# Sparse attention projections in 256, 456 and 512 columns, with merged head operations, in a two-layer hybrid trunk

## The chip, the cores and the metric

The kernel runs on one core of one Trainium2 chip. The metric is the device time in microseconds of one execution. In the profile TensorE is PE (its weight loads are PEld), VectorE is DVE, ScalarE is ACT, GpSimd is POOL and SyncE is SP. DRAM is reached by DMA queues that SP and POOL feed.

## What is computed

Two layers over 512 tokens of width 1024 in float32. In each layer one projection of the normalised input, `h @ w_in`, feeds a gated convolution, a sparse attention, a gated recurrence and a cross attention into 256 memory tokens; their outputs are lifted to width 1024, gated, added and projected, and a feed-forward block follows. The change touches the sparse attention (8 heads of 64, one key and value head, an indexer of 8 heads of 64 that picks 128 keys for each token):

```python
topk = min(TOPK_MAX, s // 4)                      # 128
q = partial_rope(rmsnorm(d_q.reshape(b, s, 8, 64), dsa_q_norm), cos, sin)
k = partial_rope(rmsnorm(d_k.reshape(b, s, 1, 64), dsa_k_norm), cos, sin)[:, :, 0]
iq = partial_rope(i_q.reshape(b, s, 8, 64), cos, sin)
ik = partial_rope(i_k.reshape(b, s, 1, 64), cos, sin)[:, :, 0]
iw = i_w * (IDX_HEADS ** -0.5)
# for each block of 128 tokens t:
rel = relu(einsum('bthd,bsd->bths', iq_t, ik) * 64 ** -0.5)
score = einsum('bths,bth->bts', rel, iw_t)        # causal: -inf behind the token
_, sel = lax.top_k(score, topk)
p = softmax(q_t . k[sel] * 64 ** -0.5)            # causal
y_b = p @ v[sel]
merged = sum(gates[:, :, n] * (branches[n] @ w_lift[n]) for n in range(4))
x = x + merged @ w_out
```

## The kernel before, in words

A float32 product is made of three matmuls (`mm3`, lines 320, 321 and 323) over operands that are split into a high and a low half: high by high, high by low, low by high. Every weight chunk of 128 x 1024 numbers is loaded by SP into `w_raw`, ACT makes `w_hi` from it (line 100 is the helper that records all ACT operations) and DVE makes `w_lo` (line 257). Matmuls add up in PSUM banks: a pool `mm` of three, a pool `tr` of three (mostly transposes), and a pool `at` of two, which holds the dot products of the attention and of the indexer.

The order of each engine's instructions is fixed before the run by a scheduler that goes through the program with a simulated timeline. What it is given is the order of generators: a string `EARLY` for each layer names steps of memory attention (m), convolution (c), the sparse projections (b), selection (s) and, in layer 1, a norm (n), and `script` runs one step for each letter. What is left of selection is woven with the lift of the memory branch (`R1`), and then `attend(0)` to `attend(3)` with the value projection of the recurrence and the lift of the convolution branch (`R2`). A manual dependency puts the dots of `attend(0)` from its third head on behind the first gate matmul.

The parts that matter here:

- `projections` walks over the sparse columns of `w_in` in five chunks of 256, 256, 200, 256 and 256 columns. For each chunk and each of four token tiles t it takes an `mm` bank, makes 24 matmuls (8 slices of the depth times three), and hands the bank to a function that copies it out (ACT), normalises and rotates the heads (DVE, `headnorm` and `rope`), turns them over (PE transposes into `tr`) and writes high and low halves (ACT and DVE).
- `select(t)` makes two dot matmuls for each of 8 heads over n = 128(t+1) columns (lines 837 and 838, into `at`), a relu on ACT into `rel` (two buffers), and adds it into `score` on DVE (lines 986 and 988). Then a predicated copy for the causal mask (line 990), sixteen rounds of a maximum (line 994, MAX8) and a match-and-replace (line 995), and the bias of the picked keys (line 998).
- `attend(t)` takes its 8 heads four at a time: two dot matmuls a head into `at`, the bias and the row maximum on DVE into `prob` (line 853, in the trace CUSTOM_DVE_ANT_0, in the order ISA), an exponential on ACT, a reciprocal on DVE (line 856), a scaling copy on ACT, then transposes on PE (line 867). The dots of heads 2 and 3 can't start before line 853 of heads 0 and 1 has emptied the two `at` banks.
- The gates of a lift are evicted at line 661, and merged at lines 222 and 678.

Of the kernel before, what the change touches and what calls it, by code (L numbers as in the profile page):

```python
# [12 lines left out]
F32 = mybir.dt.float32  # L13
# [31 lines left out]
EARLY = ["mmbcmmbmmbsccsmmcsssmsccbmb", "mnmbmmbmmcbsccsmmcsssmsccbmb"]  # L45
# [26 lines left out]
def hybrid_trunk(ctx: ExitStack, tc: tile.TileContext, x, mem, positions, norm_mix, w_in, conv_w,  # L72
# [557 lines left out]
    def mixer(l, h, norms, cm):  # L630
# [197 lines left out]
        with pool_("dsa") as dp:  # L828
# [60 lines left out]
            with pool_("idx") as ip:  # L889
# [4 lines left out]

                def rope(u, heads, t):
# [3 lines left out]
                    a = ip.tile([P, 4, ROT], F32, name="rope_a", bufs=2)[:, :heads]  # L899
                    b = ip.tile([P, 4, ROT], F32, name="rope_b", bufs=2)[:, :heads]  # L900
# [6 lines left out]
                def headnorm(u, heads, gain):  # L907
                    sq = ip.tile([P, 4, HD], F32, name="hn_sq", bufs=1)[:, :heads]
# [8 lines left out]
                def heads_T(dst, h0, u, heads, t):  # L917
                    ps = tr_ps()[:, :heads * HD]
                    for i in range(heads // 2):
                        pe.transpose(ps[:, i * P:(i + 1) * P], u[:, i * P:(i + 1) * P], ident)  # L920
                    ps = ps.rearrange("p (a b) -> p a b", b=P)
# [7 lines left out]
                def unit(ps, t, c0, heads):  # L929
                    u = ip.tile([P, 4, HD], F32, name="unit", bufs=3)[:, :heads]  # L930
                    with tc.high_priority(offset=AHEAD):
                        A(u.rearrange("p a b -> p (a b)"), ps[:, c0:c0 + heads * HD], AF.Copy, scale=r_t[:, t:t + 1])
                    return u

                def twin(ps, t, c0, norm, dst):
                    u = ip.tile([P, 2, HD], F32, name="twin", bufs=4)
                    with tc.high_priority(offset=AHEAD):
                        A(u[:, 0, :], ps[:, c0:c0 + HD], AF.Copy, scale=r_t[:, t:t + 1])
                    if norm:
                        headnorm(u[:, 0:1], 1, gk_b[l])  # L940
                    rope(u[:, 0:1], 1, t)
                    dve.tensor_copy(u[:, 1, :], u[:, 0, :])
                    ps = tr_ps()[:, :P]
                    pe.transpose(ps, u.rearrange("p a b -> p (a b)"), ident)
# [4 lines left out]
                def iq_part(ps, t, c0, heads, h0):  # L949
                    u = unit(ps, t, c0, heads)  # L950
                    rope(u, heads, t)
                    heads_T(iqS, h0, u.rearrange("p a b -> p (a b)"), heads, t)

                def c_kv(ps, t):
                    with tc.high_priority(offset=AHEAD):
                        A(vt[:, t, :], ps[:, 64:128], AF.Copy, scale=r_t[:, t:t + 1])
                    twin(ps, t, 0, True, kS)
                    iq_part(ps, t, 128, 2, 0)

                def c_iq(ps, t):  # L960
                    iq_part(ps, t, 0, 4, 2)

                def c_last(ps, t):
                    with tc.high_priority(offset=AHEAD):
                        A(iw[:, t, :], ps[:, 192:200], AF.Copy, scale=r8_t[:, t:t + 1])
                    iq_part(ps, t, 0, 2, 6)
# [695 lines left out]
```

## Time and profile before

| what | value |
|---|---|
| median of 3 runs | 1968.37 us (1968.28 to 1968.54) |
| profiled execution, its own time | 1968.67 us |
| its span, first to last instruction | 1966.7 us |
| PE busy | 1959.5 us, 100% of the span |
| DVE busy | 1482.2 us, 75% |
| ACT busy | 1180.1 us, 60% |
| POOL busy | 235.7 us, 12% |
| matmul and transpose instructions | 9879 |

The busy shares are averages over the span, so the profile is read by stages: which engine the last instruction's chain goes through, what PE waited for, and then the timeline of the stretch in which the change lies (82 to 332 us in layer 0 and 1037 to 1265 us in layer 1). In a timeline row a matmul's own time is longer than the distance to the next start, because matmuls overlap; the rate of PE is the distance from start to start.

### The profile page before, as it was taken

How to read it: one execution, taken by the hardware profiler on the slowest of the kernel's cores; microseconds unless marked ns; L12 is line 12 of the kernel's file. 1: busy time of each engine (PE TensorE's matmuls, PEld its weight loads, DVE VectorE, ACT ScalarE, POOL GpSimd, SP SyncE). 2: the span in 40 equal slices, each digit the busy share in tenths (PEclk: the TensorE clock that was granted, in tenths of full speed). 3: DMA queues.
4: the chain of work that ended last, by engine and by line, in shares of the span. 5: the costliest groups of instructions: out<-in, count | busy, mean ns of one | idle time of the engine just before them, and what ended most of it. 6: DMA issues, size and time to landing. Idle time of an engine off the chain costs nothing.

```text
span 1966.7 us, 27345 instructions
## 1 busy us (share of the span) xinstructions
PE 1959.5 (100%) x9879; PEld 1641.7 (83%) x9879; DVE 1482.2 (75%) x2769; ACT 1180.1 (60%) x2038; POOL 235.7 (12%) x288
## 2 busy tenths in 40 slices
PE   9999999999999999999999999999999999999999
PEld 7898988878888888888889898888888888888887
DVE  7869997657876677776877889965678667867777
ACT  6653655866765556655655455477667656556464
POOL 1011111111111111100001111111111110111000
PEclk9999999999999999999999999999999999999999
DMA  8677766767677888885676666676766789888654
GB/s 303 205 175 174 169 165 174 166 142 172 167 207 183 235 233 254 248 239 187 203 220 169 170 150 166 161 188 156 171 172 168 205 198 250 256 264 236 215 185 138
DMA packets 224278, 385.27 MB, mean 196 GB/s; under 512 B 13194, under 2 KB 120272, under 8 KB 223888
## 3 DMA queue, kind: packets, MB, share of 16 engines
q1 hardware_dynamic: 165056, 244.16, 39.1%
q0 software_dynamic: 52192, 132.81, 32.9%
q10 hardware_dynamic: 6896, 6.58, 1.0%
q8 instruction: 77, 1.26, 0.3%
q14 instruction: 57, 0.47, 0.1%
HBM read 368.81 MB, written 140.51 MB: 259 GB/s over the span
## 4 chain that ended last, share of the span: by engine, by line
PE 99%; DVE 0%; ACT 0%; issue 0%; DVEq 0%; ACTq 0%
PE mm L320 25%; PE mm L321 24%; PE mm L323 24%; PE at L320 4%; PE at L323 4%; PE at L321 4%; PE tr L320 2%; PE tr L323 1%; PE tr L321 1%; PE at L838 1%; PE tr L878 1%; PE tr L867 1%; PE tr L1554 1%; PE at L837 1%; PE tr L804 0%; PE at L1136 0%
## 5 line engine op out<-in xcount | busy, mean ns | idle before, releaser
L100 ACT ACTIVATE w_hi<-w_raw 128x1024 fp32r<-128x1024 f32 (+1 forms) x435 | 457.6, 1054 | 353.7 <-PE mm L321 115.3
L320 PE MATMUL mm<-h_hi,w_hi 128*128 128x512 f32 x960 | 376.9, 394 | 0.6 <-DVE zg L1053 0.6
L321 PE MATMUL mm<-h_lo,w_hi 128*128 128x512 f32 x960 | 377.0, 393 | 0.0
L323 PE MATMUL mm<-h_hi,w_lo 128*128 128x512 f32 x960 | 371.9, 393 | 0.0
L1265 DVE TENSOR_TENSOR w_lo<-w_raw,w_hi 128x1024 fp32r<-128x1024 f32 x211 | 256.2, 1217 | 130.1 <-ACT w_hi L100 129.3
L257 DVE TENSOR_TENSOR w_lo<-w_raw,w_hi 128x1024 fp32r<-128x1024 f32 (+1 forms) x224 | 271.8, 1215 | 89.7 <-ACT w_hi L100 87.8
L1280 POOL DMA_DIRECT2D up_sums<-in_ffn_w_up_dram x120 | 121.4, 1012 | 822.9 <-DMA up_sums<-in_ffn_w_up_dram 540.1
L320 PEld LDWEIGHTS mm<-h_hi,w_hi 128*128 128x128 f32 x960 | 180.4, 188 | 37.0 <-issue 1.0
L321 PEld LDWEIGHTS mm<-h_lo,w_hi 128*128 128x128 f32 x960 | 180.4, 188 | 36.4 <-issue 0.2
L323 PEld LDWEIGHTS mm<-h_hi,w_lo 128*128 128x128 f32 x960 | 180.2, 188 | 36.4 <-issue 0.2
L321 PE MATMUL mm<-w_lo,h_hi 128*128 128x256 f32 (+2 forms) x568 | 187.6, 330 | 0.3 <-DVE w_lo L257 0.3
L323 PE MATMUL mm<-w_hi,h_lo 128*128 128x256 f32 (+2 forms) x568 | 187.7, 331 | 0.0
L320 PE MATMUL mm<-w_hi,h_hi 128*128 128x256 f32 (+2 forms) x568 | 181.4, 331 | 0.0
L321 PEld LDWEIGHTS mm<-w_lo,h_hi 128*128 128x128 f32 x568 | 107.8, 190 | 10.4 <-DVE w_lo L257 0.6
L323 PEld LDWEIGHTS mm<-w_hi,h_lo 128*128 128x128 f32 x568 | 107.7, 190 | 9.4
L320 PEld LDWEIGHTS mm<-w_hi,h_hi 128*128 128x128 f32 x568 | 107.5, 190 | 9.6 <-ACT w_hi L100 0.2
L1280 POOL DMA_DIRECT2D w_sums<-in_ffn_w_down_dram x66 | 62.2, 943 | 335.9 <-DMA w_sums<-in_ffn_w_down_dram 187.0
L100 ACT ACTIVATE prob<-prob,small 128x128 f32<-128x128 f32 (+3 forms) x128 | 68.8, 555 | 21.9 <-DVE small L853 16.1
L321 PE MATMUL mm<-y_lo,w_hi 128*128 128x512 f32 x192 | 75.8, 395 | 0.0
L323 PE MATMUL mm<-y_hi,w_lo 128*128 128x512 f32 x192 | 75.4, 392 | 0.0
L320 PE MATMUL mm<-y_hi,w_hi 128*128 128x512 f32 x192 | 75.3, 393 | 0.0
L321 PE MATMUL mm<-w_lo,a_hi 128*128 128x512 f32 x160 | 63.2, 395 | 0.0
(502 smaller groups left out, 4213.3 us busy)
## 6 DMA issues: line engine op xcount, KB each, us to landing
w_raw<-in_w_in_dram SPq DMA_DIRECT2D x144, 512.0 KB, 4.8
up_sums<-in_ffn_w_up_dram POOLq DMA_DIRECT2D x120, 512.0 KB, 6.7
w_raw<-up_sums SPq DMA_DIRECT2D x80, 512.0 KB, 5.0
w_raw<-in_ffn_w_up_dram SPq DMA_DIRECT2D x60, 512.0 KB, 4.8
w_sums<-in_ffn_w_down_dram POOLq DMA_DIRECT2D x54, 512.0 KB, 6.4
up_sums<-up_sums POOLq DMA_DIRECT2D x40, 512.0 KB, 5.1
w_raw<-in_w_lift_dram SPq DMA_DIRECT2D x32, 512.0 KB, 4.5
w_raw<-in_ffn_w_down_dram SPq DMA_DIRECT2D x24, 512.0 KB, 5.4
```

Of the source, the lines that this page charges most:

```text
L100: i = act.activation(dst, src, func, **kw)
L257: i2 = dve.tensor_sub(lo, raw, f(hi))
L320: made += [pe.matmul(ps, ah, bh, start=first, stop=False, skip_group_check=more), pe.matmul(ps, ah, bl, start=False, stop=False, skip_grou ...
L321: pe.matmul(ps, ah, bl, start=False, stop=False, skip_group_check=more)]
L323: made += [pe.matmul(ps, al, bh, start=False, stop=last, skip_group_check=more)]
L837: return [pe.matmul(ps, q[:, hh, s], k[0][:, :n], start=True, stop=False), pe.matmul(ps, q[:, hh, s], k[1][:, :n], start=False, stop=True)]
L838: pe.matmul(ps, q[:, hh, s], k[1][:, :n], start=False, stop=True)]
L867: turn = pe.transpose(pp[:, (2 * e + i) * P:(2 * e + i + 1) * P], probs[2 * i + e][:, b * P:(b + 1) * P], ident)
L878: i = pe.matmul(pv[e * HD:(e + 1) * HD, c], vt[:, b, :], pt[:, b, e * 2 * P:(e + 1) * 2 * P], start=b == 0, stop=b == t)
L1265: two = A(hi, raw, AF.Copy), dve.tensor_sub(lo, raw, f(hi))
L1280: i = nc.gpsimd.dma_start(dst, src, **kw)
L1554: turns.extend(pe.transpose(ps[:, t * P:(t + 1) * P], us[t][:, j * P:(j + 1) * P], ident) for t in range(NT))
```

## The change

The sparse projections become three chunks: 256 columns (key, value and two index heads) as before, one of 456 columns (six index heads, the index key, the index weights) and one of 512 (all queries). The two wide chunks are made slice by slice of the depth for all four token tiles at once, over four accumulators (the three `mm` banks and one of `tr`), in an order that dependencies hold. Each is copied out whole, with one operation for a tile, into a tile `wide`, of which there are four; `select` takes its `rel` from the same four. Normalising, rotating, turning and splitting run on all heads of a tile at once. `EARLY` is changed: the 512 block stands ahead of three memory steps, and each of its four token tiles is a step of its own.

```diff
-EARLY = ["mmbcmmbmmbsccsmmcsssmsccbmb", "mnmbmmbmmcbsccsmmcsssmsccbmb"]
+EARLY = ["mmbmcmcbmmmsccbmscmbscmbsbbss", "mnmbmcmcbmmmsccbmscmbscmbsbbss"]
...
-    def tokens_wide(ws, a, kt, pss, first=0):
-
-        k0 = 0
+    def tokens_wide(ws, a, kt, pss, first=0, in_turn=False):
+
+        k0, behind_part = 0, None
         for w in ws:
             for ks, _, _ in w.parts[0 if k0 else first:]:
+                made = []
                 for t, ps in enumerate(pss):
                     for k in ks:
-                        mm3(ps, pair(a, k0 + k, slice(t * P, (t + 1) * P)), w.at(k), k0 + k == 0, k0 + k == kt - 1)
+                        made += mm3(ps, pair(a, k0 + k, slice(t * P, (t + 1) * P)), w.at(k), k0 + k == 0, k0 + k == kt - 1)
+                for i in made if in_turn and behind_part is not None else []:
+                    tc.add_manual_dep(i.ins, behind_part.ins.name, order, reason="part by part")
+                behind_part = made[-1]
...
+                def wide():
+                    return ip.tile([P, S], F32, name="wide", bufs=4)
...
-                    a = ip.tile([P, 4, ROT], F32, name="rope_a", bufs=2)[:, :heads]
-                    b = ip.tile([P, 4, ROT], F32, name="rope_b", bufs=2)[:, :heads]
+                    a = ip.tile([P, 8, ROT], F32, name="rope_a", bufs=1)[:, :heads]
+                    b = ip.tile([P, 8, ROT], F32, name="rope_b", bufs=1)[:, :heads]
...
+                def index_out(ps, t):
+                    u = wide()
                     with tc.high_priority(offset=AHEAD):
-                        A(iw[:, t, :], ps[:, 192:200], AF.Copy, scale=r8_t[:, t:t + 1])
...
+                        A(u[:, :7 * HD], ps[:, :7 * HD], AF.Copy, scale=r_t[:, t:t + 1])
+                        A(iw[:, t, :], ps[:, 7 * HD:7 * HD + 8], AF.Copy, scale=r8_t[:, t:t + 1])
+                    return u
+
+                def index_heads(u, t):
+                    w = by_head(u)
+                    rope(w[:, :7], 7, t)
+                    dve.tensor_copy(w[:, 7, :], w[:, 6, :])
+                    ps = turn_heads(u, 4)
+                    twin_to(ikS, ps[:, 3 * P:], t)
+                    heads_to(iqS, 2, ps[:, :3 * P], 6, t)
...
+                def query_heads(u, t):
+                    w = by_head(u)
+                    headnorm(w, 8, gq_b[l])
+                    rope(w, 8, t)
+                    heads_to(qS, 0, turn_heads(u, 4), 8, t)
...
-                        rel = ip.tile([P, S], F32, name="rel", bufs=2)[:, :n]
+                        rel = wide()[:, :n]
...
-                    for c0, n, handle in ((C_DK, 256, c_kv), (C_DK + 256, 256, c_iq), (C_DK + 512, 200, c_last),
-                                          (C_DQ, 256, c_q(0)), (C_DQ + 256, 256, c_q(1))):
-                        w = wchunk(w_in[l][:, c0:c0 + n], KD, n)
-                        for t in range(NT):
-                            ps = mm_ps()[:, :n]
-                            tokens(w, h, t, ps)
-                            handle(ps, t)
+                    w = wchunk(w_in[l][:, C_DK:C_DK + 256], KD, 256)
+                    for t in range(NT):
+                        ps = mm_ps()[:, :256]
+                        tokens(w, h, t, ps)
+                        key_heads(key_out(ps, t), t)
+                    yield
+                    for c0, n, evict, handle, each in ((C_DK + 256, 456, index_out, index_heads, False),
+                                                       (C_DQ, 512, query_out, query_heads, True)):
+                        pss = [mm_ps()[:, :n] for _ in range(MM_BUFS)] + [tr_ps()[:, :n]]
+                        tokens_wide([wchunk(w_in[l][:, c0:c0 + n], KD, n)], h, KD, pss, in_turn=True)
+                        us = [evict(ps, t) for t, ps in enumerate(pss)]
+                        for t, u in enumerate(us):
+                            if each:
+                                yield
+                            handle(u, t)
                         yield
```

Lines behind the changed functions shift: 837 and 838 become 841 and 842, 853 becomes 857, 856 becomes 860, 867 becomes 871, 661 becomes 665, 988 becomes 1002, 990 becomes 1004, 994 and 995 become 1008 and 1009, 998 becomes 1012, and the matmuls of `mm3` stand at 324, 325 and 327.

The scheduler makes a new order from this. PE differs in two stretches only, one in each layer. At the first index block of layer 0, PE had in the kernel before, where a 200-column tile is mixed with memory attention (`at<-mk,qg` and `at<-mpt,mv`):

```order
L323 MATMUL at<-mk,qg_lo 128x256
L320 MATMUL mm<-w_hi,h_hi 128x200
L321 MATMUL mm<-w_lo,h_hi 128x200
L321 MATMUL at<-mpt_lo,mv 128x256
L323 MATMUL at<-mpt_hi,mv 128x256
```

and it now has one chunk of 456 columns, a token tile after the other (the fourth accumulator is named `tr`):

```order
L327 MATMUL mm<-w_hi,h_lo 128x456
L324 MATMUL mm<-w_hi,h_hi 128x456
L325 MATMUL mm<-w_lo,h_hi 128x456
L327 MATMUL mm<-w_hi,h_lo 128x456
L808 MATMUL tr<-ident,mprob 128x128 x2
L324 MATMUL tr<-w_hi,h_hi 128x456
L325 MATMUL tr<-w_lo,h_hi 128x456
```

What moved there is which matmuls stand together: the index block no longer comes in three visits.

Further on PE makes the last two dots of `select(3)`, layer 0. In the kernel before they stand among gate matmuls (`mm<-h_hi,w_hi`), with 195 instructions of PE between them and the dots of heads 2 and 3 of `attend(0)`:

```order
L320 MATMUL mm<-h_hi,w_hi 128x512
L321 MATMUL mm<-h_lo,w_hi 128x512
L323 MATMUL mm<-h_hi,w_lo 128x512
L837 MATMUL at<-ik_hi,iqS 128x512
L838 MATMUL at<-ik_lo,iqS 128x512
```

Now they stand among the matmuls of the value projection of the recurrence (`mm<-w_hi,h_hi`), with 86 instructions of PE between them and the same dots of `attend(0)`:

```order
L324 MATMUL mm<-w_hi,h_hi 128x512
L841 MATMUL at<-ik_hi,iqS 128x512
L842 MATMUL at<-ik_lo,iqS 128x512
L325 MATMUL mm<-w_lo,h_hi 128x512
L327 MATMUL mm<-w_hi,h_lo 128x512
L841 MATMUL at<-ik_hi,iqS 128x512
L842 MATMUL at<-ik_lo,iqS 128x512
L325 MATMUL tr<-w_lo,h_hi 128x512
```

What stands between is 50 matmuls of 512 columns, four dots (heads 0 and 1 of `attend(0)`), 32 more matmuls of 512 columns, and then, in this order, the dots of heads 2 and 3 and the first transpose of a probability:

```order
L324 MATMUL mm<-h_hi,w_hi 128x512
L325 MATMUL mm<-h_lo,w_hi 128x512
L841 MATMUL at<-k_hi,qS 128x128
L842 MATMUL at<-k_lo,qS 128x128
L841 MATMUL at<-k_hi,qS 128x128
L842 MATMUL at<-k_lo,qS 128x128
L871 MATMUL tr<-ident,prob 128x128
```

The distance between the index dots and the attention dots moved; their sequence did not. In layer 1 the same rows stand with the same 86 instructions between.

On DVE, layer 0, the rounds that follow those dots stood among weight halves (`w_lo`) and gates in the kernel before:

```order
L988 SCALAR_TENSOR_TENSOR score<-rel,iw,score 128x512 x2
L990 COPY_PREDICATED score<-future,neg 128x128
L994 MAX m_3361<-score 128x8
L995 MATCH_REPLACE score<-m_3361,score 128x512
L994 MAX m_3364<-score 128x8
L995 MATCH_REPLACE score<-m_3364,score 128x512
L257 TENSOR_TENSOR w_lo<-w_raw,w_hi 128x1024
L994 MAX m_3367<-score 128x8
L661 TENSOR_TENSOR gate<-mm,rstd 128x512
```

Now the sixteen rounds have nothing between them; the first of them and the last, with what follows, are:

```order
L1002 SCALAR_TENSOR_TENSOR score<-wide,iw,score 128x512 x2
L1004 COPY_PREDICATED score<-future,neg 128x128
L1008 MAX m_2933<-score 128x8
L1009 MATCH_REPLACE score<-m_2933,score 128x512
L1008 MAX m_2936<-score 128x8
```

```order
L1009 MATCH_REPLACE score<-m_3090,score 128x512
L1012 TENSOR_SCALAR bias_786<-score 128x512
L857 ISA prob,small<-at,causal_bias 128x128
L857 ISA small 128x1
L857 ISA prob,small<-at,causal_bias 128x128
L857 ISA small 128x1
L257 TENSOR_TENSOR w_lo<-w_raw,w_hi 128x1024 x3
L860 RECIPROCAL small<-small 128x1 x2
```

So the weight halves and gates that stood between the rounds are now ahead of them, and the first two `prob` of `attend(0)` follow the bias as they did.

## Rows read from the trace of the kernel before

**Rows 1.** The page, parts 1 and 2: busy time and granted clock.
```profile
PE 1959.5 (100%) x9879; PEld 1641.7 (83%) x9879; DVE 1482.2 (75%) x2769; ACT 1180.1 (60%) x2038; POOL 235.7 (12%) x288
...
PEclk9999999999999999999999999999999999999999
```

**Rows 2.** The page, part 4: the chain that ended last, by engine.
```profile
PE 99%; DVE 0%; ACT 0%; issue 0%; DVEq 0%; ACTq 0%
```

**Rows 3.** PE's waits, all of them: us in total, times, longest.
```profile
PE tr L148 <- DVE one L130: 1.2, 1, 1.2
PE mm L539 <- ACT w_hi L100: 0.7, 1, 0.7
PE mm L320 <- DVE zg L1053: 0.6, 1, 0.6
PE mm L321 <- DVE w_lo L257: 0.3, 1, 0.3
```

**Rows 4.** Timeline of PE: start us, us, engine, line, operation, tiles, columns.
```profile
99.31 0.28 PE L323 MATMUL mm<-w_hi,h_lo 128*128 128x256 f32 x1
...
104.59 0.29 PE L321 MATMUL mm<-w_lo,h_hi 128*128 128x256 f32 x1
```

**Rows 5.** The same, 200, 384 and 512 columns.
```profile
125.92 0.27 PE L323 MATMUL mm<-w_hi,h_lo 128*128 128x200 f32 x1
...
130.50 0.28 PE L321 MATMUL mm<-w_lo,h_hi 128*128 128x200 f32 x1
...
208.20 0.34 PE L837 MATMUL at<-ik_hi,iqS 128*128 128x384 f32 x1
208.37 0.34 PE L838 MATMUL at<-ik_lo,iqS 128*128 128x384 f32 x1
...
305.83 0.39 PE L321 MATMUL mm<-w_lo,h_hi 128*128 128x512 f32 x1
...
316.71 0.39 PE L323 MATMUL tr<-w_hi,h_lo 128*128 128x512 f32 x1
```

**Rows 6.** Timeline of all engines: last dots of select(3), layer 0, to the first round.
```profile
285.83 0.39 PE L837 MATMUL at<-ik_hi,iqS 128*128 128x512 f32 x1
...
286.49 0.60 ACT L100 ACTIVATE rel<-at 128x512 f32<-128x512 f32 x1 [0.56 <-PE at L838]
...
287.12 0.75 DVE L988 SCALAR_TENSOR_TENSOR score<-rel,iw,score 128x512 f32<-128x512 f32 x1 [0.24 <-ACT rel L100]
...
288.30 0.70 DVE L994 MAX8 m<-score 128x8 f32<-128x512 f32 x1
```

**Rows 7.** Timeline of DVE: four rounds with nothing between (first and fifth maximum).
```profile
306.72 0.69 DVE L994 MAX8 m<-score 128x8 f32<-128x512 f32 x1
...
312.78 0.70 DVE L994 MAX8 m<-score 128x8 f32<-128x512 f32 x1
```

**Rows 8.** Timeline of DVE: the bias and the first probabilities of attend(0).
```profile
320.63 0.72 DVE L998 TENSOR_SCALAR bias<-score 128x512 f32<-128x512 f32 x1
321.27 0.27 DVE L853 CUSTOM_DVE_ANT_0 prob<-at,causal_bias 128x128 f32<-128x128 f32 x1
...
321.68 2.38 DVE L257 TENSOR_TENSOR w_lo<-w_raw,w_hi 128x1024 fp32r<-128x1024 f32 x2
323.98 0.36 DVE L856 RECIPROCAL small<-small 128x1 f32<-128x1 f32 x2
```

**Rows 9.** Timeline of ACT and then of PE: what comes of those probabilities.
```profile
325.55 0.69 ACT L100 ACTIVATE prob<-prob,small 128x128 f32<-128x128 f32 x2
...
330.09 0.22 PE L837 MATMUL at<-k_hi,qS 128*128 128x128 f32 x1
...
331.47 0.27 PE L867 MATMUL tr<-ident,prob 128*128 128x128 f32 x1
```

**Rows 10.** Timeline of PE at the start of the program, 128 columns each.
```profile
1.16 3.99 PE L148 MATMUL tr<-ones_h 128*128 128x128 f32 x18 [1.16 <-DVE one L130]
4.98 0.38 PE L460 MATMUL at<-ident,mem_in 128*128 128x128 f32 x2
```

More of the change, by code (lines that the diff above doesn't have):

```diff
@@ L893, in mixer, with by_head @@
                 iw = ip.tile([P, NT, 8], F32, name="iw")
+                def wide():
+                    return ip.tile([P, S], F32, name="wide", bufs=4)
+                def by_head(u):
+                    return u.rearrange("p (a b) -> p a b", b=HD)
                 def rope(u, heads, t):
@@ L907, in headnorm @@
                 def headnorm(u, heads, gain):
-                    sq = ip.tile([P, 4, HD], F32, name="hn_sq", bufs=1)[:, :heads]
+                    sq = by_head(ip.tile([P, S], F32, name="hn_sq", bufs=1))[:, :heads]
                     A(sq, u, AF.Square, scale=HD ** -0.5)
@@ L915, in headnorm, with turn_heads, heads_to @@
                     dve.tensor_mul(u, u, gain[:, None, :].to_broadcast([P, heads, HD]))
-                def heads_T(dst, h0, u, heads, t):
-                    ps = tr_ps()[:, :heads * HD]
-                    for i in range(heads // 2):
+                def turn_heads(u, n):
+                    ps = tr_ps()[:, :n * P]
+                    for i in range(n):
                         pe.transpose(ps[:, i * P:(i + 1) * P], u[:, i * P:(i + 1) * P], ident)
+                    return ps
+                def heads_to(dst, h0, ps, heads, t):
                     ps = ps.rearrange("p (a b) -> p a b", b=P)
@@ L927, in heads_T, with twin_to @@
                         dve.tensor_sub(d[HD:P], src, f(d[0:HD]))
[L929 to L944, printed above, removed]
+                def twin_to(dst, ps, t):
                     s = slice(t * P, (t + 1) * P)
@@ L960, in c_iq, with key_out @@
[L960 to L975 removed]
+                def key_out(ps, t):
+                    u = wide()[:, :4 * HD]
+                    with tc.high_priority(offset=AHEAD):
+                        A(vt[:, t, :], ps[:, HD:2 * HD], AF.Copy, scale=r_t[:, t:t + 1])
+                        A(u[:, HD:2 * HD], ps[:, 0:HD], AF.Copy, scale=r_t[:, t:t + 1])
+                        A(u[:, 2 * HD:], ps[:, 2 * HD:4 * HD], AF.Copy, scale=r_t[:, t:t + 1])
+                    return u
@@ new lines, in key_heads @@
+                def key_heads(u, t):
+                    w = by_head(u)
+                    headnorm(w[:, 1:2], 1, gk_b[l])
+                    rope(w[:, 1:4], 3, t)
+                    dve.tensor_copy(w[:, 0, :], w[:, 1, :])
+                    ps = turn_heads(u, 2)
+                    twin_to(kS, ps[:, :P], t)
+                    heads_to(iqS, 0, ps[:, P:], 2, t)
+                def index_out(ps, t):
+                    u = wide()
+                    with tc.high_priority(offset=AHEAD):
+                        A(u[:, :7 * HD], ps[:, :7 * HD], AF.Copy, scale=r_t[:, t:t + 1])
+                        A(iw[:, t, :], ps[:, 7 * HD:7 * HD + 8], AF.Copy, scale=r8_t[:, t:t + 1])
+                    return u
@@ new lines, in index_heads, with query_out @@
+                def index_heads(u, t):
[5 more added lines that the diff above has]
+                    heads_to(iqS, 2, ps[:, :3 * P], 6, t)
+                def query_out(ps, t):
+                    u = wide()
+                    with tc.high_priority(offset=AHEAD):
+                        A(u, ps, AF.Copy, scale=r_t[:, t:t + 1])
+                    return u
@@ L977, in select @@
+                def query_heads(u, t):
+                    w = by_head(u)
+                    headnorm(w, 8, gq_b[l])
+                    rope(w, 8, t)
+                    heads_to(qS, 0, turn_heads(u, 4), 8, t)
                 def select(t):
@@ L992, in select @@
                     for i in range(TOPK // 8):
-                        m8 = ip.tile([P, 8], F32, name="m8", bufs=2)
+                        m8 = ip.tile([P, 16], F32, name="m8", bufs=2)[:, :8]
                         dve.max(m8, score)
```

16 lines of the change are left out of this document (removed).

## The prediction

> **What bounds the kernel now.** I read the page's busy times first: PE is busy for the whole span at the full granted clock [rows 1]. Then the chain that ended last, which goes through PE for 99% of its length [rows 2], and the list of PE's waits, which adds up to 2.8 us in 1966.7 [rows 3]. So the kernel is a string of matmuls, and only two things count: what the string itself takes, and whether another engine makes PE stand. A faster DVE or ACT is worth nothing as long as it is not late. The profiled execution took 1968.67 us, 0.30 above the median of 1968.37; the sum is made against the former and set down by 0.3 at the end.
>
> **The matmuls of the projections.** I take the distance from start to start, not the duration, since matmuls overlap. From one row to the other lie 44 starts in 5.28 us: 0.120 us for 256 columns [rows 4]. In the same way 41 starts in 4.58 us give 0.112 for 200 columns, 48 in 10.88 give 0.227 for 512, and the two neighbouring rows give 0.17 for 384 [rows 5]. Narrow matmuls are dear: 200 columns cost nearly as much as 256.
>
> A layer had 16 tile-chunks (four chunks by four token tiles) of 24 matmuls with 256 columns, and 4 with 200: 384 x 0.120 + 96 x 0.112 = 56.8 us. Now it has 96 with 256, 96 with 456 and 96 with 512. No row has 456 columns; it lies between 0.17 (384) and 0.227 (512), and a straight line between these gives 0.202, which I take since the matmul rows rise with their columns. So 96 x (0.120 + 0.202 + 0.227) = 52.7 us, 4.1 less a layer and **-8.2 us** in two. The bounds by 0.17 and 0.227 are -14.4 and -3.4. The transposes stay at 40 a layer: nothing.
>
> **The merged operations.** Fewer and larger DVE and ACT operations for normalising, rotating and splitting. On PE's path they can win no more than the 2.8 us of all its waits [rows 3], none of which names a tile of the projections; I take 0. The four accumulators of a wide chunk have to be copied out before the next user of the banks starts. The chunk goes slice by slice, so the four tiles' last slices end one after the other, and a copy of 512 columns is one ACT operation (0.60 us for the relu of as many [rows 6]): between 0 and 4 x 0.60 us for each of four chunks, 0 to 9.6 us. I take 0, because the row it is nearest to, an eviction to ACT, names no wait of PE before. SP's weight loads keep their number of bytes, and their order follows PE's; PE's waits for weights were 0.7 and 0.3 us [rows 3]: 0.
>
> **What moved, and the wait that it makes.** The order of instructions is fixed, so the place where something is late can be counted. In layer 0 the last two dots of `select(3)` stood 195 PE instructions ahead of the dots of heads 2 and 3 of `attend(0)`; now it is 86. These attention dots need the two `at` banks back, which the first two `prob` operations on DVE empty, and these are queued on DVE behind everything that `select(3)` does after its last dots. That chain, from the start of the last head's dots:
>
> - To the first maximum: dots at 285.83, relu at 286.49, score at 287.12, maximum at 288.30 [rows 6]: 2.47 us.
> - Sixteen rounds. Four rounds with nothing between take 312.78 - 306.72 = 6.06 us [rows 7], 1.515 each: 24.24 us. All sixteen now stand without anything between.
> - The bias to the first `prob`, 320.63 to 321.27, and that one's 0.27 us [rows 8]: 0.91 us.
>
> Together 27.6 us. PE from the same start has the two dots (2 x 0.227), 82 matmuls of 512 columns (18.6 us) and four dots of 128 columns (0.4; no more than the 0.12 of 256 columns each [rows 4]), 19.5 us, and then stands until 27.6: a **wait of 8.1 us**. Before, PE came to these dots at 330.09 [rows 9], when the `prob` of 321.27 [rows 8] was 8.6 us past. It is this slack that is spent.
>
> Right behind the four dots comes the first transpose of a `prob`. It needs the ACT copy, this the reciprocal, and DVE now has three weight halves ahead of the reciprocal. The first `prob` starts at 27.35 of this count; the halves start 0.41 behind it (321.68 to 321.27 [rows 8]), at 27.76; two take 2.30 until the reciprocal (323.98 [rows 8]), so three take 3.45: 31.2. One of the two reciprocals (0.18 [rows 8]) and one of the two copies (0.35 [rows 9]) make 31.8. PE is through with its dots at 27.6 + 0.45 = 28.1: a **second wait of 3.7 us**. Both are on PE's path, with nothing to hide them: the next matmuls are queued behind them on PE, and the rest of the kernel behind these. After that PE keeps 16 matmuls between one set of dots and the next transposes while DVE has little queued, so I see no third one.
>
> Layer 1 has the same rows with the same distance, so it is 2 x (8.1 + 3.7) = **+23.6 us**. The bounds: the first wait is counted from durations of this trace and is good to half a microsecond; the second lies between 0 (weight halves overlapped in some way) and 3.7 plus the 1.06 us of an ACT weight half that could stand ahead of the copy.
>
> **The clock after the waits.** PE never stands long in this trace but once: until 1.16 us at the start. The 18 matmuls of 128 columns that follow take 4.98 - 1.16 = 3.82 us, 0.212 each [rows 10], where 256 columns take 0.120 later: this is the lower of the two levels, 1.2 GHz against 2.4, and up to half of it, 1.9 us, is lost (by the 0.120, 1.7). The only wait of 0.7 us [rows 3] is too short to tell what a longer one does. So a wait of 8 us costs between 0 and 1.9 us on top; I take 1.8, since the start is the nearest row to an engine that stood for long. For two layers **+3.6 us**.
>
> The Trainium skill, page "TensorE: Matmul & The Clock Gate", section "Why this matters for your kernels", speaks for the upper end: it says that an idle gap between bursts of matmuls sends the clock back to its half rate. By that rule the sum has the term, and without it the sum is lower by 3.6 us; no run here shows it yet.
>
> **The sum.** 1968.67 - 8.2 + 23.6 + 3.6 = 1987.7, less 0.3 for the median: **1987.4 us**, 1.0% slower.
>
> **Rivals.**
>
> - *No clock, or half of the second wait gone.* Without the clock it is 1983.8. If the weight halves don't delay the reciprocal, the second wait goes too: 1968.4 - 8.2 + 16.2 = 1976.4. For it: DVE may be offered the reciprocal at another time than I count. Against: its order is fixed, with three halves ahead.
> - *The evictions of the wide chunks.* A block of four accumulators that ends all at once makes the steps behind it wait for ACT: up to 9.6 us on top, 1997. For it: the block takes all of `mm`. Against: the tiles end one after the other, 6 matmuls apart, 1.4 us, and one copy takes 0.6.
> - *The other side, faster.* The wait does not come about because the rounds are done in time. From the last dots PE offers 19.5 us; less 2.5 ahead and 0.9 behind, 16.1 are left for sixteen rounds. It decides at 1.0 us a round, against 1.515 measured. Then the matmuls' gain stands alone: 1968.4 - 8.2 = 1960.2, faster by 0.4%. Against: the undisturbed rounds take 1.515 [rows 7], and the change leaves their operations and widths as they are.
>
> **How the numbers follow.** The forecast with both waits, with or without the clock (1983 to 1990): 0.70. Only the first wait, or a much cheaper 456 (1975 to 1983): 0.12. Evictions or more DVE lateness (1990 to 1998): 0.08, beyond that 0.02. No wait, 1960: 0.06; some remainder of it within 0.2%: 0.02. The range from 1976 to 1997 leaves out the faster side and the far ends, somewhat over 1 in 10. A measurement of this kernel can tell about 0.2% from no change, 3.9 us. Faster by more than that: 0.06; within it: 0.02 and a little of the neighbours, 0.03; slower: 0.91.
>
> **What would show it.** In the profile of the changed kernel the list of PE's waits has two pairs of new rows, one pair a layer: `at<-k_hi,qS` at line 841 waiting for DVE's `prob` of line 857, some 8 us, and `tr<-ident,prob` at line 871 waiting for ACT's copy, some 4 us, near 328 us and near 1290 us. DVE's timeline ahead of them shows sixteen rounds of 1.5 us in a row. The granted clock dips behind them if the clock term is right. The 456-column matmuls start 0.20 us apart. I am wrong if PE waits in other places, above all behind the wide chunks, or if PE's waits remain at 3 us.

## The result and the profile after

The changed kernel takes 1992.38 us in the median (1991.71 to 1993.16), where the kernel before takes 1968.45 beside it: a ratio of 1.0119, 95% interval 1.0105 to 1.0133. It is slower by 24 us. The profiled execution took 1991.71, with a span of 1989.7, 23.0 above that of before.

First the page of the changed kernel: the busy time of the engines, the granted clock in 40 slices, and the chain that ended last by engine.

```profile
PE 1959.2 (98%) x9495; PEld 1626.9 (82%) x9495; DVE 1468.1 (74%) x2569; ACT 1171.7 (59%) x1950; POOL 236.1 (12%) x288
...
PEclk9999998999999999999999999989999999999999
...
PE 96%; DVE 3%; ACT 0%; issue 0%; DVEq 0%; ACTq 0%
```

Against [rows 1, 2]: PE is busy as long as before, with 384 instructions fewer, but no longer for the whole span. The clock has a dip in two slices, and 3% of the chain now goes through DVE. The list of PE's waits (us in total, times, longest) says where, against [rows 3]:

```profile
PE at L841 <- DVE small L857: 15.9, 2, 8.0
PE tr L871 <- ACT prob L100: 6.0, 2, 3.0
...
PE at L324 <- ACT mpt_hi L100: 0.9, 2, 0.5
...
PE tr L808 <- DVE mprob L806: 0.3, 1, 0.3
```

The first two rows are new and make 21.9 us. The `mpt_hi` and `mprob` rows are new and small. The rows left out are the four of before, within 0.1 us.

The timeline of PE shows the place, in layer 0 and then in layer 1 (start, us, engine, line, operation, tiles, columns; in brackets the idle time ahead and what ended it):

```profile
308.38 0.39 PE L841 MATMUL at<-ik_hi,iqS 128*128 128x512 f32 x1
...
336.01 0.47 PE L841 MATMUL at<-k_hi,qS 128*128 128x128 f32 x1 [7.97 <-DVE small L857]
...
340.13 0.47 PE L871 MATMUL tr<-ident,prob 128*128 128x128 f32 x1 [3.01 <-ACT prob L100]
340.26 5.19 PE L327 MATMUL mm<-h_hi,w_lo 128*128 128x512 f32 x16
345.29 0.39 PE L324 MATMUL mm<-y_hi,w_hi 128*128 128x512 f32 x1
...
1299.79 0.47 PE L841 MATMUL at<-k_hi,qS 128*128 128x128 f32 x1 [7.96 <-DVE small L857]
...
1303.92 0.48 PE L871 MATMUL tr<-ident,prob 128*128 128x128 f32 x1 [3.01 <-ACT prob L100]
```

And the timeline of DVE in the same stretch of layer 0: the first of the sixteen rounds, the bias behind the last, the first probability, the weight halves, the reciprocals.

```profile
311.03 0.69 DVE L1008 MAX8 m<-score 128x8 f32<-128x512 f32 x1
...
335.32 0.43 DVE L1012 TENSOR_SCALAR bias<-score 128x512 f32<-128x512 f32 x1
335.66 0.28 DVE L857 CUSTOM_DVE_ANT_0 prob<-at,causal_bias 128x128 f32<-128x128 f32 x1
...
336.08 3.49 DVE L257 TENSOR_TENSOR w_lo<-w_raw,w_hi 128x1024 fp32r<-128x1024 f32 x3
339.49 0.22 DVE L860 RECIPROCAL small<-small 128x1 f32<-128x1 f32 x2
```

Read together: the last index dots of `select(3)` start at 308.38 and no longer at 285.83 [rows 6]; sixteen rounds take 335.32 - 311.03 = 24.29 us; the first probability comes at 335.66 and no longer at 321.27 [rows 8]. PE is at the attention dots at 336.01 - 7.97 = 328.04, 2.05 us earlier than the 330.09 of before [rows 9]. The first probability comes 14.4 us later and PE 2.05 earlier, 16.4 together: 8.8 of it used up the slack that there was (330.09 - 321.27), and the other 7.6, with the 0.35 us from the start of that probability to the dots, are the wait of 7.97.

Where the 23.0 us went, from these rows:

| part | us |
|---|---|
| first wait, 7.97 + 7.96 | +15.9 |
| first dots to first transpose, 4.12 and 4.13 us instead of the 0.45 that four dots were counted with | +7.3 |
| the 16 matmuls behind (345.29 - 340.26 = 5.03 us; 6.02 in layer 1, by the window shown further down; 16 x 0.227 = 3.63) | +3.8 |
| matmuls of the projections: 96 x (0.120 + 0.2075 + 0.227) = 53.2 us a layer for 56.8 | -7.1 |
| a short stand in memory attention, below | +2.3 |
| not assigned | +0.8 |

The short stand is at the first dots of `select(2)` in layer 0 and at the same place in layer 1. On PE's timeline in layer 0:

```profile
243.39 0.48 PE L327 MATMUL mm<-h_hi,w_lo 128*128 128x512 f32 x1
244.32 0.39 PE L324 MATMUL at<-mpt_hi,mv 128*128 128x256 f32 x1 [0.45 <-ACT mpt_hi L100]
```

A matmul of 512 columns behind four transposes starts 0.93 us ahead of the next one; in such a place 0.31 is usual (263.82 to 264.13 in the same timeline). The steps behind it are late too: 0.22 us for a matmul of 256 columns instead of 0.12, and 0.74 for four transposes that take 0.36 elsewhere. From 243.04 to 246.09 the steps take 3.05 us, and by the distances of such steps elsewhere some 1.9: about 1.15 us a layer, and the same steps in layer 1 take as long.

### The profile page after: what moved, and what is told of

Read it like the earlier page. It is cut to its first block, busy times and chain, and to the rows that moved or that the text cites. A ratio compares the mean times of both kernels' runs of the same rounds, so it can differ in the third digit from the quotient of the medians.

```text
span 1989.7 us, 26286 instructions
## 1 busy us (share of the span) xinstructions
PE 1959.2 (98%) x9495; PEld 1626.9 (82%) x9495; DVE 1468.1 (74%) x2569; ACT 1171.7 (59%) x1950; POOL 236.1 (12%) x288
## 4 chain that ended last, share of the span: by engine, by line
PE 96%; DVE 3%; ACT 0%; issue 0%; DVEq 0%; ACTq 0%
PE mm L327 23%; PE mm L324 23%; PE mm L325 23%; PE at L324 4%; PE at L325 4%; PE at L327 4%; PE tr L324 2%; PE tr L327 2%; PE tr L325 2%; DVE score L1009 1%; DVE m L1008 1%; PE tr L871 1%; PE tr L882 1%; PE tr L1576 1%; PE at L841 1%; PE at L842 1%
## 5 line engine op out<-in xcount | busy, mean ns | idle before, releaser
L327 PE MATMUL mm<-h_hi,w_lo 128*128 128x512 f32 x960 | 375.9, 398 | 0.0
L1302 POOL DMA_DIRECT2D up_sums<-in_ffn_w_up_dram x120 | 121.5, 1012 | 827.7 <-DMA up_sums<-in_ffn_w_up_dram 531.5
L327 PE MATMUL mm<-w_hi,h_lo 128*128 128x512 f32 (+2 forms) x408 | 152.0, 373 | 0.0
L325 PE MATMUL mm<-w_lo,h_hi 128*128 128x512 f32 (+2 forms) x408 | 151.7, 372 | 0.3 <-DVE w_lo L257 0.3
L324 PE MATMUL mm<-w_hi,h_hi 128*128 128x512 f32 (+2 forms) x408 | 145.6, 372 | 0.0
L325 PEld LDWEIGHTS mm<-w_lo,h_hi 128*128 128x128 f32 x408 | 76.8, 188 | 12.8 <-DVE w_lo L257 0.6
L324 PEld LDWEIGHTS mm<-w_hi,h_hi 128*128 128x128 f32 x408 | 76.8, 188 | 12.3 <-ACT w_hi L100 0.2
L327 PEld LDWEIGHTS mm<-w_hi,h_lo 128*128 128x128 f32 x408 | 76.8, 188 | 11.8
```

What stands on the lines that cost most here:

```text
L324: made += [pe.matmul(ps, ah, bh, start=first, stop=False, skip_group_check=more), pe.matmul(ps, ah, bl, start=False, stop=False, skip_grou ...
L325: pe.matmul(ps, ah, bl, start=False, stop=False, skip_group_check=more)]
L327: made += [pe.matmul(ps, al, bh, start=False, stop=last, skip_group_check=more)]
L1302: i = nc.gpsimd.dma_start(dst, src, **kw)
```

## The experiments

Two things are to be told apart. The first is the mechanism: my theory is that the order of DVE makes the loss, so that it shrinks by what is taken out of the rounds, and goes when the attention's probabilities need not stand behind them. The rival is that the wide blocks cost the time (evictions, banks), so that it stays whatever becomes of that order. The second is the clock: does it fall because PE stood for 8 us, or would the shorter second wait do it alone? All diffs are against the changed kernel except where it says before.

### Sixteen rounds cut to thirteen

```diff
-                    for i in range(TOPK // 8):
+                    for i in range(TOPK // 8 - 3 * (t == 3)):
```

> The changed kernel with thirteen of the sixteen rounds in select(3): the last three maxima and replacements are left out, so the last 128 tokens attend to 24 keys fewer. The order is the same otherwise, but for one transpose of layer 0 that stands two matmuls earlier, so that its two waits become one. Theory (PE waits for the end of the chain of rounds): 3 x 1.515 = 4.55 us less of waiting in each layer, the first wait of layer 1 falls from 8.0 to 3.5, the sum of the two in layer 0 from 11.0 to 6.4, 9.1 us in all: 1992.4 - 9.1 = 1983.3 us (1981 to 1985). Rival (something else than the rounds ends the wait, as a weight or a copy on ACT): 1990 to 1992 us.

It took 1983.59 us (1982.48 to 1985.81), ratio 1.0078 [1.0061, 1.0095]. The span went from 1989.7 to 1981.0, 8.7 us less for six rounds of 1.515 us (9.1). PE's waits:

```profile
PE tr L871 <- ACT prob L100: 10.9, 2, 7.8
PE at L841 <- DVE small L857: 3.4, 1, 3.4
```

In layer 0 the order now has a transpose ahead of the dots, so that one wait of 7.8 us stands for the pair. DVE's rounds are on the path, nearly one for one.

### More matmuls in front of the dots

32 matmuls of 512 columns are added in each layer, ahead of the dots of heads 2 and 3: the first two products of the first two gates are made twice and added up twice, so these gates come from doubled terms.

```diff
-        runs = [(part, ks) for part in range(2) for ks, _, _ in w.parts] if late_lo else [(None, ks) for ks, _, _ in w.parts]
-        for part, ks in runs:
+        runs = [(part, ks, again) for part, again in ((0, 0), (0, 1), (1, 0)) for ks, _, _ in w.parts] if late_lo else [(None, ks, 0) for ks, _, _ in w.parts]
+        for part, ks, again in runs:
...
-                    last = mm3(ps, w.tile(k, j), pair(a, k0 + k), k0 + k == 0, k0 + k == kt - 1, part=part)[-1]
+                    last = mm3(ps, w.tile(k, j), pair(a, k0 + k), k0 + k == 0 and not again, k0 + k == kt - 1, part=part)[-1]
...
-                    tc.add_manual_dep(i.ins, first_gates[0].ins.name, order, reason="gates first")
+                    tc.add_manual_dep(i.ins, first_gates[1].ins.name, order, reason="gates first")
```

(The first transposes of `attend(0)` are held behind the same gate.)

> The changed kernel with 32 matmuls of 512 columns more in each layer, set on PE just ahead of the dots of heads 2 and 3 of attend(0), where PE stands for 8.0 us; the order of everything else is the same. The matmuls repeat the first two products of the first two gates, so those gates are computed from doubled terms. They are 32 x 0.227 = 7.26 us of PE work a layer, 14.5 us in two. Theory (PE stands there for DVE's rounds): the first wait shrinks from 8.0 to 0.7 us, the second stays at 3.0, DVE's times don't move, and the clock no longer falls, so the time goes down by the clock's cost alone, some 4.6 us: 1988 us (1986 to 1993). Rival (the wait is not what the kernel is longer by, PE's work is): 1992.4 + 14.5 = 2007 us.

It took 1991.66 us (1991.4 to 1993.2), ratio 1.0115 [1.0098, 1.0132]: 64 x 0.227 = 14.5 us more work on PE for nothing. PE's waits, then its timeline in layer 0, then the window behind the second wait (PE and PEld busy with counts, DVE, ACT, POOL, granted clock, DMA share, GB/s):

```profile
PE tr L871 <- ACT prob L100: 6.9, 2, 3.5
PE at L841 <- DVE small L857: 1.4, 2, 0.7
```

```profile
336.32 0.33 PE L841 MATMUL at<-k_hi,qS 128*128 128x128 f32 x1 [0.71 <-DVE small L857]
...
340.45 0.47 PE L871 MATMUL tr<-ident,prob 128*128 128x128 f32 x1 [3.46 <-ACT prob L100]
340.58 5.99 PE L327 MATMUL mm<-h_hi,w_lo 128*128 128x512 f32 x16
346.41 0.40 PE L324 MATMUL mm<-y_hi,w_hi 128*128 128x512 f32 x1
```

```profile
340.40:346.50 6.10, 6.05 (x18) 4.84 (x19) 0.03 (x3) 2.71 (x6) 1.14 (x1) 0.62 1.08 286
```

The first wait falls from 15.9 to 1.4, by the 14.5 that was put in: PE had been idle for that long. I had expected some 4 us below the changed kernel, because the clock would stay up. It did not. The dots ran at full pace this time (0.11 apart), but after the second stand of 3.46 us the 16 matmuls took 5.83 us for 3.63, and the granted clock of the stretch was 0.62; in layer 1 they took 6.46. So with 0.7 us of standing in place of 8.0 the clock's cost was 2.2 and 2.8 us, not less than the 1.4 and 2.4 of the changed kernel: the second wait is enough for it, and the 8 us are not needed.

### The order of before, with selection late

On the kernel before, `EARLY` alone, with the selection steps moved behind the others:

```diff
-EARLY = ["mmbcmmbmmbsccsmmcsssmsccbmb", "mnmbmmbmmcbsccsmmcsssmsccbmb"]
+EARLY = ["mmbcmmbmmbccmmcbsmbscsss", "mnmbmmbmmcbccmmcbsmbscsss"]
```

> The kernel before, five chunks and unmerged operations, with EARLY altered so that the selection starts later. The last dots of select(3) then stand 67 PE instructions, 14.6 us, ahead of the dots of heads 2 and 3 of attend(0), with sixteen rounds in a row on DVE, 27.6 us. Theory (the order alone makes the loss): a wait of 13.0 us in each layer at those dots, 1 to 3 us more behind them, and 2.5 of the clock: 1968.4 + 33 to 37 = 2001 to 2005 us, less by a few where DVE gains elsewhere. Rival (the wait needs the wide blocks or the shared tiles): 1968 to 1972.

It took 2008.11 us (2007.68 to 2008.95), ratio 1.0196 [1.0180, 1.0212]. PE's waits:

```profile
PE tr L867 <- ACT prob L100: 19.2, 2, 17.3
PE at L837 <- DVE small L853: 12.9, 1, 12.9
```

(The new string names one `m`, one `c` and one `s` fewer; steps that it doesn't name run behind it.) The old chunks, with not one wide block, get the same two waits when selection comes late, and longer ones, 32.1 us instead of 21.9. The time is 3 us above the 2001 to 2005 that I expected; that part was not followed up. (The 17.3 is layer 0, where a transpose stands ahead of the dots.) So the blocks are not needed for the loss; the place of selection makes it.

### Selection earlier in the changed kernel

If selection is what is late, an earlier place for it should give the time back. Three orders of the changed kernel: one `s` moved forward (the expectation speaks of two steps, but one letter of the string moves); several; and all, with the query steps last.

```diff
-EARLY = ["mmbmcmcbmmmsccbmscmbscmbsbbss", ...
+EARLY = ["mmbmcmcbsmmmccbmscmbscmbsbbss", ...
```

> The changed kernel with only the string EARLY altered: the first two steps of selection are moved ahead, the blocks and merged operations stay. The dots of select(3) then stand 105 PE instructions, 23.8 us, ahead of the dots of heads 2 and 3 of attend(0), against 19.5; DVE has one weight half among the sixteen rounds, 28.8 us in all against 27.6. Theory: first wait 4.9 us in each layer, the waits behind it (for a weight half and for the copied probability) 3.6 together, so 1992.4 - 2 x (8.0 + 3.0 - 4.9 - 3.6) = 1987.4 us, and down to 1983 if the shorter wait costs less of the clock. Rival (the wide blocks themselves cost the time, wherever the selection stands): 1992 us.

```diff
+EARLY = ["mmbmcmcbmmmssccbmsscmbsscmbbb", ...
```

> The changed kernel with only EARLY altered, selection further ahead of the queries: 29.0 us of PE work (layer 1: 29.7) between the last dots of select(3) and the dots of heads 2 and 3 of attend(0), against 28.8 us (29.4) that DVE needs. Theory: no first wait; the second, for the copied probability, stays at about 3 us a layer, since three weight halves still stand ahead of the reciprocal: 1992.4 - 16 - 1 to 4.6 of the clock = 1972 to 1976 us. Rival (the blocks cost it): 1992 us.

```diff
+EARLY = ["mmbbcmcmsmmmsccsmscmsscmbbbbb", ...
```

> The changed kernel with only EARLY altered: all steps of selection ahead of the steps that handle the queries. 68 us of PE work between the last dots of select(3) and the dots of heads 2 and 3 of attend(0), against 44.7 that DVE needs; the reciprocals stand ahead of the weight halves. Theory: neither wait, no fall of the clock, and only the blocks' gain of some 7 us and the 2 us of PE's waits behind the blocks are left: 1961 to 1965 us, faster than the kernel before. Rival (the blocks cost time by themselves): over 1985 us. A new wait may come where attend(0) needs the queries, which are handled later: up to 1970 us.

| order | median us | ratio to before |
|---|---|---|
| one step earlier | 1990.99 (1990.35 to 1991.69) | 1.0112 [1.0097, 1.0128] |
| several | 1995.82 (1995.40 to 1995.98) | 1.0137 [1.0121, 1.0152] |
| queries last | 2013.18 (2012.32 to 2014.78) | 1.0226 [1.0211, 1.0241] |

All three missed, and by their times alone they speak for the rival. The rows of PE's waits that differ most, one kernel after the other in this order:

```profile
PE at L841 <- DVE small L857: 9.3, 2, 4.6
PE tr L808 <- DVE mprob L806: 5.8, 3, 2.8
```

```profile
PE tr L808 <- DVE mprob L806: 8.0, 3, 3.8
...
PE at L841 <- DVE small L857: 2.3, 2, 1.4
```

```profile
PE tr L808 <- DVE mprob L806: 18.7, 6, 4.1
PE tr L930 <- DVE wide L959: 7.0, 3, 3.6
```

The row of the attention dots goes down much as I said: 9.3 (4.6 at most, 4.9 expected), then 2.3 where none was expected, then gone. But another row grows as it shrinks: the transposes of memory attention wait for `mprob`, DVE's division of its probabilities. DVE's timeline in the second of these kernels shows what stands ahead of one of them:

```profile
255.22 0.68 DVE L794 TENSOR_REDUCE small<-at 128x2 f32<-128x512 f32 x1
...
256.20 0.56 DVE L1008 MAX8 m<-score 128x8 f32<-128x384 f32 x1
...
257.91 0.56 DVE L1008 MAX8 m<-score 128x8 f32<-128x384 f32 x1
258.39 0.60 DVE L806 TENSOR_SCALAR mprob<-mprob,small 128x256 f32<-128x256 f32 x2
```

Between the maximum of a memory softmax (255.22) and its division (258.39) DVE does a round of selection and the maximum of the next, 1.74 us of operations, beside a mask and a sum for the queries, and PE stands 3.81 us until the first division is done. How much of the 3.81 is the selection's was not separated. DVE's order is fixed; moving the rounds forward moved the wait to another user of DVE, and in the third order the new rows (18.7 and 7.0) cost more than the attention's waits did (21.9). Whether some other order of the changed kernel would cost nothing wasn't tried.

### Probabilities that don't wait for selection

The row of line 857 reads `prob<-at,causal_bias`: the probabilities of `attend(0)` use no bias that selection makes. Yet in the traces of both kernels none stands ahead of the bias that ends `select(3)`. What ties them is memory. `score` and its maxima lie in a pool `idx`, and `prob` lies in a pool that takes over its place, so no `prob` can be written before the last round has used `score`. Two lines move these two tiles to the pool that lives on:

```diff
-                    score = ip.tile([P, S], F32, name="score", bufs=1)[:, :n]
+                    score = dp.tile([P, S], F32, name="score", bufs=1)[:, :n]
...
-                        m8 = ip.tile([P, 16], F32, name="m8", bufs=2)[:, :8]
+                        m8 = dp.tile([P, 16], F32, name="m8", bufs=2)[:, :8]
```

> The changed kernel with two tiles moved: score and the maxima lie in the pool that lives to the end of attention, no longer in the pool of the index tiles, on whose release the tiles of attend wait. PE's order up to the dots of heads 2 and 3 of attend(0) is the same, 19.5 us behind the last dots of select(3). DVE's order is not: the first two prob operations stand between the sixth and the seventh of the sixteen rounds, with the weight halves and reciprocals right behind, and the rounds go on among the later steps of attention. Theory (PE's 22 us of waits come of what is queued ahead on DVE, not of the amount of work): both waits vanish and the clock doesn't fall, 1992.4 - 22 - 4 to 5 = 1966 us (1963 to 1971), a little under the kernel before. Rival (DVE can't do the work of this stretch in time, in whatever order): the waits turn up at other places of attention and the time stays over 1980.

It took 1967.46 us (1966.93 to 1968.36), ratio to before 0.9991 [0.9982, 1.0000], 25 us below the changed kernel. The fences show first those of PE's waits that the kernel before does not have (without the row of `mprob`, 0.3), then DVE's timeline around the first probability, then a window over the place (columns as above):

```profile
PE tr L871 <- ACT pt L100: 0.9, 2, 0.5
PE at L324 <- ACT mpt_hi L100: 0.9, 2, 0.5
...
PE tr L882 <- ACT pt L100: 0.6, 2, 0.3
```

```profile
320.84 0.69 DVE L1008 MAX8 m<-score 128x8 f32<-128x512 f32 x1
321.44 0.27 DVE L857 CUSTOM_DVE_ANT_0 prob<-at,causal_bias 128x128 f32<-128x128 f32 x1
...
321.72 0.67 DVE L1009 MATCH_REPLACE8 score<-m,score 128x512 f32<-128x512 f32 x1
```

```profile
320.00:345.00 25.00, 25.00 (x122) 20.77 (x121) 24.10 (x64) 15.88 (x37) 2.66 (x4) 1.00 0.81 206
```

The probability now stands inside a round, between its maximum and its replacement, at 321.44 instead of 335.66. Both waits are gone, PE is busy for the whole window, and the granted clock is 1.00. The wide blocks and the merged operations are all still in this kernel, so the two waits and their clock are the whole loss: the rival that the blocks cost it is out. Its span is 1.8 us below before, where the matmuls alone give 7.1. The stand in memory attention (2.3) and a new one at two `pt` copies (the rows at L871 and L882, with slow starts around them some 1.4 us a layer) take the rest back.

The same two lines in the kernel before, where nothing waits there:

```diff
-                    score = ip.tile([P, S], F32, name="score", bufs=1)[:, :n]
+                    score = dp.tile([P, S], F32, name="score", bufs=1)[:, :n]
...
-                        m8 = ip.tile([P, 8], F32, name="m8", bufs=2)
+                        m8 = dp.tile([P, 8], F32, name="m8", bufs=2)
```

> The kernel before with the same two tiles moved. Theory: it had no wait there (8.6 us to spare), so nothing is gained: 1968.4 us, within 0.2%, up to 1971 if a round now stands ahead of something that PE needs. Rival (the move of the tiles is a gain of its own): 1960 or less.

It took 1969.64 us (1968.59 to 1970.88), ratio 1.0002 [0.9993, 1.0011]: no difference. The two lines are worth nothing by themselves; they are worth 25 us where selection is late.

### The index block alone

The block of 456 columns and its merged operations, with the queries again as two chunks of 256 (through the tiles `wide`), and an order like that of before:

```diff
-EARLY = ["mmbmcmcbmmmsccbmscmbscmbsbbss", "mnmbmcmcbmmmsccbmscmbscmbsbbss"]
+EARLY = ["mmbcmmmmbsccsmmcsssmsccbmb", "mnmbmmmmcbsccsmmcsssmsccbmb"]
...
+                    for q in range(2):
+                        w = wchunk(w_in[l][:, C_DQ + q * 256:C_DQ + (q + 1) * 256], KD, 256)
+                        for t in range(NT):
+                            ps = mm_ps()[:, :256]
+                            tokens(w, h, t, ps)
+                            u = wide()[:, :256]
```

> The index block of 456 columns and its merged operations as in the changed kernel; the queries in two chunks of 256 columns, a tile after the other, as before the change, and EARLY as before with one projection step less. The selection starts as early as before: 55 us of PE work between the last dots of select(3) and the dots of heads 2 and 3 of attend(0), against 41 that DVE needs. Matmuls: 96 x (0.120 + 0.112 - 0.2075) = 2.4 us less a layer, with 0.2075 for 456 columns from the changed kernel. Theory: no wait, 1968.4 - 4.7 = 1963.7 us (1962 to 1967 with small waits for the evictions). Rival (the wide block costs by itself): 1968 us or more.

It took 1995.14 us (1988.91 to 1997.65), ratio 1.0125 [1.0110, 1.0140]. PE's first waits:

```profile
PE mm L324 <- ACT wide L100: 6.2, 6, 1.6
PE at L324 <- DMA mv<-kv: 3.2, 1, 3.2
```

The wait of attention is gone here too, but this kernel has a fault of its own: eight query tiles share four `wide` with `select`, and PE waits for their copies. The time is 31 us above the 1963.7 that I expected. PE's waits add up to 20.8 us (2.8 before), 8.6 of which name `wide`, and the rest of the 31 was not assigned. The run doesn't isolate the block, and what the block of 456 columns is worth alone stays open.

## Why the prediction was right, and by how much it was off

The forecast was 1987.4 us in a range of 1976 to 1997; measured were 1992.38. The sign and the mechanism were right. But 1983 to 1990 had been given to this story, with 0.70, and the measured time lies above it, in the band that was kept for late evictions and more lateness of DVE, with 0.08. What put it there were small misses that nearly all have the same sign, none of them at the wide chunks' banks; the band was too narrow for them. By its steps:

- **The first wait.** Predicted 8.1 us in each layer, measured 7.97 and 7.96, at the lines and times named. The sixteen rounds took 24.29 for 24.24. The ends of the chain were each 0.2 us off, 2.65 for 2.47 ahead of the rounds and 0.69 for 0.91 behind them, and cancel: 27.63 for 27.6, which is luck in the last two tenths.
- **The second wait.** Predicted 3.7, listed as 3.0. As a distance it was right: from the first dots to the first transpose 31.8 - 27.6 = 4.2 us were predicted, 4.12 and 4.13 measured. The four dots ran at the low clock and filled 0.7 us more of it, so the wait in the list is shorter, at the same cost. Three weight halves ahead of the reciprocals (3.49 us for 3.45) are in the row at 336.08.
- **The clock.** Predicted 1.8 us in each layer; measured behind the transposes 1.4 and 2.4, 3.8 for 3.6 together. That the sums are so near is partly luck: the price was taken from 18 matmuls of 128 columns at the start of the program, and with more matmuls in front the same 16 matmuls lost 2.2 and 2.8. The second wait would have brought it without the first.
- **The matmuls.** Predicted -8.2, by the measured pace -7.1. The starts of 456 columns are 0.2075 us apart, not 0.202; the straight line from 384 to 512 was a little low. Two layers of 96 of them make 1.1 us.
- **Evictions and small waits.** Predicted 0 with a bound of 9.6, measured about 2.3: not behind the wide chunks' banks, where I looked for it, but at memory attention, where a product waits for ACT's `mpt_hi`. I had named PE waits in other places as a sign of being wrong, and this is a small one.
- **The merged operations.** 0, and no run separates them: with the waits away, the kernel ends within 0.1% of before, and whether the small stands that eat up the matmuls' 7.1 us come of the merged operations or of the order stays open.

Between the profiled executions, 1991.71 is 4.0 us above the 1987.7 that the sum gave before the median was taken: 1.1 from the 456 columns, 2.3 from memory attention, 0.8 that no row was found for, and -0.2 from the waits (23.2 for 23.6) and the clock (3.8 for 3.6) together. The other 1.0 us lies between profile and median (the median fell 0.7 above the profile, where I had set it 0.3 below).

What the prediction did not see is why the probabilities stand behind selection. I took the order of DVE as given and wrote that they "are queued on DVE behind everything that `select(3)` does". That holds for the kernel as it is. But they don't depend on it, and two lines undo it. The row `prob<-at,causal_bias` stood in front of me [rows 8].

The rival without the clock (1983.8) fell to the granted clock and the 3.8 us, and the one without the second wait (1976.4) to the second wait's row. The rival of the other side, that the rounds are done in time (1960.2), fell to the rounds, which took 24.29 / 16 = 1.52 us each. The evictions' rival (1997) fell to the kernel with `score` moved, which has the same evictions and 1967.46.

That the clock falls is in the windows of the changed kernel (columns as above): the first dots to the transpose, the matmuls behind, and those of layer 1.

```profile
336.01:340.13 4.12, 1.11 (x4) 0.92 (x5) 4.10 (x11) 1.31 (x6) 0.10 (x1) 0.50 0.73 148
340.26:345.29 5.03, 5.03 (x17) 4.03 (x18) 0.21 (x2) 2.96 (x8) 1.19 (x1) 0.73 1.00 305
1304.05:1310.07 6.02, 6.02 (x18) 4.76 (x18) 2.25 (x4) 3.40 (x9) 0.00 (x0) 0.59 1.01 231
```

The granted clock is 0.50, the 1.2 GHz level, from the dots to the transpose, and a mean of 0.73 and 0.59 over the 16 matmuls. The Trainium skill, page "TensorE: Matmul & The Clock Gate", section "Why this matters for your kernels", says that an idle gap between bursts of matmuls sends the clock back to its half rate. These rows agree with it, and the kernel in which no such gap is left has 1.00 in its window.

One reading of the prediction is not borne out as it stands. It called the start of the program the lower level by the pace of its matmuls, 0.212 us apart [rows 10]. In the kernel before, the granted clock that the profile gives for that stretch is 1.00 (columns as above):

```profile
2.00:4.00 2.00, 2.00 (x11) 2.00 (x11) 0.00 (x0) 1.49 (x2) 1.91 (x6) 1.00 0.79 232
```

So the profile doesn't show the low level there; what bears the price out is the changed kernel, where dots of 128 columns at a granted 0.50 start 0.21 us apart (336.28, 336.49 and 336.70) and at full pace 0.11.

## What to carry to other kernels

An operation that is late behind another on an engine need not depend on it: compare what it reads with what it stands behind, and where they have nothing in common look for memory that the two share. Then a change of two lines can be worth more than another order: 25 us here, while of three other orders of the same steps the best gave 1.4 back (its interval and that of the changed kernel overlap), and the others took 3 and 21 more, with new waits for another user of the same engine. And a merged block that is cheaper by its own matmuls (7.1 us) has to be priced with the distances that it changes around it, counted in instructions on PE and in rounds on DVE. Here the 7.1 us did not come out even with the two lines: 1967.46 us, with an interval of the ratio to before that reaches 1.0000.

## What was unexpected of the hardware

- The clock falls after a shorter stand than 8 us: in the kernel with more matmuls in front PE stood 0.71 us, made four dots, stood 3.46 us, and the next 16 matmuls took 5.83 us instead of 3.63, at a granted clock of 0.62. What the fall costs varies for the same code: 1.4 us in layer 0 and 2.4 in layer 1 of the changed kernel, and 2.2 and 2.8 in the kernel with more matmuls in front.
- 456 columns start 0.2075 us apart, here between the 0.17 of 384 and the 0.227 of 512 [rows 5], nearer to the upper than a straight line says. On PE's timeline of the changed kernel:

```profile
128.71 0.37 PE L327 MATMUL mm<-w_hi,h_lo 128*128 128x456 f32 x1
...
131.82 0.37 PE L327 MATMUL tr<-w_hi,h_lo 128*128 128x456 f32 x1
```

From 128.71 to 131.82 there are 15 starts in 3.11 us, 0.2073 each.
